# When the second gather, the first scatter and the embedding's product are written among the experts

## The chip, the cores and the metric

The kernel runs on one core of one Trainium2 chip. The metric is the device time of one execution, in microseconds (us), as the median of several runs. TensorE does the matrix products, VectorE (DVE), ScalarE (ACT) and GpSimd (POOL) the rest, and SyncE (SP) issues the transfers from the memory of the chip.

## The reference

Two layers of an encoder over 512 tokens of width 1024, in float32. Each layer has a token mixer, then a routed mixture of 16 experts, then a gated embedding. The change touches the last two:

```python
logits = jnp.einsum('bsd,de->bse', h, w_router)
aff = jax.nn.softmax(logits, axis=-1)
vals, idx = lax.top_k(aff.transpose(0, 2, 1), cap)      # cap = 64 tokens for each expert
xg = h[bidx, idx]
h1 = jnp.einsum('becd,edf->becf', xg, w1)               # w1, w3, w2: 1024 x 1024 for each expert
h3 = jnp.einsum('becd,edf->becf', xg, w3)
out = jnp.einsum('becf,efd->becd', jax.nn.silu(h1) * h3, w2) * vals[..., None]
x = x + jnp.zeros_like(h).at[bidx, idx].add(out)
...
ple_gate = jax.nn.sigmoid(rmsnorm(x, norm_ple[i]) @ ple_gate_w[i])
x = x + ple_gate * (p[i] @ ple_w[i])                    # p: 512 x 256, ple_w: 256 x 1024
```

Each expert has 12 MB of weights, and they are read once in each layer.

## The kernel before, in words

Tokens lie on the 128 partitions in four chunks, `x[:, c, :]`. The weights of an expert come as 1 MB tiles (`w_tile`, L565), four for each of `w1` and `w3`, into a ring of 15 slots (tag `s8`) that other tiles share. SP issues the loads in one queue, in order; a load waits until its slot is free.

The expert stage of a layer goes like this.

- Experts 0 to 3 (L806) each gather their own tokens (`gather_one`), do their products (`hidden`) and the product with `w2` (`down`), whose results stay in `obs`, one slot of the ring.
- `gather(ga, 4, 6)` (L820) gathers the tokens of experts 4 to 9 into `xgA`. It makes a mask `sel` from the positions (L710) and then, in eight steps, one for each 128 columns of `x`, splits a scaled `x` into a high and a low half (`xh` on ACT, `xl` on DVE, two buffers each), multiplies both with the mask on TensorE (eight matmuls, L720) and copies the result out of its bank.
- The loop over experts 4 to 15 (L835) calls `hidden` for each. Per expert: for `w1` and then `w3`, eight values of `k`, two halves (L738). The trace has two records for each of these 32 matmuls, 64 for an expert and 8 for a weight tile. After a quarter of an expert's products, `between` transposes the expert before it (L753) into the slot `kept`. Then tanh on ACT (L744) and two operations on DVE (L745, L746).
- Ahead of expert 7 (`GATHER_B`, L836) stands the gather of experts 10 to 15 into `xgB`. Behind expert 7 stand two calls of `scatter` (L846), which add the outputs in `obs` to `x`; each calls `where`, which makes a mask `sv` on DVE (L690), transposes it on TensorE (L693) into a bank of tag `T`, and multiplies it with the affinities (L698). `T` has two banks, and the transposes of `between` use it too.
- Behind expert 11 (`PLE_AT`, L847) stands the product of the embedding, `pw`: it loads `p` and two halves of `ple_w` through the same ring (L828), splits each into a high half (ACT, L95) and a low half (DVE, L831) and does eight groups of six matmuls (L150).
- After expert 15 come `where` for the last six pairs (L865) and the products with `w2` of experts 4 to 15 (L900) with their scatter.

The order of the instructions of each engine isn't that of the text. A planner goes through the whole program with a model of the chip's times; among the instructions whose inputs and slots are there it gives an engine the one that stands first in the program. The slots of one tag are handed out in the program's order. `issue_after` queues instructions behind a given one.

Of the kernel before, what the change touches and what calls it, by code (L numbers as in the profile page):

```python
# [10 lines left out]
F32 = mybir.dt.float32  # L11
# [8 lines left out]
P = 128  # L20
D = 1024
S = 512
NE = 16
CAP = 64
NEARLY = 6

ONE = 4
NA_ = 6
RING = 15
BLOCKED = 4  # L30
EARLY_END = ONE * 8 + BLOCKED * 4 - 4
GATHER_B = 7

PLE_AT = 11
SPL = 3
GTB = 1
S0B = 2
# [26 lines left out]
def trunk(ctx, tc, a, out, L=2, dbg=None):  # L64
# [15 lines left out]
    x = const.tile([P, 4, D], F32, name="x")  # L80
# [13 lines left out]
    def acopy(o, i, scale=1.0):  # L94
        sc.activation(o, i, AF.Copy, scale=scale)  # L95

    def bc(ap, n):
        return ap.unsqueeze(2).to_broadcast([P, ap.shape[1], n])
# [83 lines left out]
    for l in range(L):  # L182
# [263 lines left out]
        with tc.tile_pool(name=f"na{l}", bufs=2, side="right", reuse_waits="tile") as ap_:  # L446
# [3 lines left out]
            for pr in range(4):  # L450
                pts = []
                for hh_ in range(2):
# [4 lines left out]
                    for c in range(4):  # L457
# [16 lines left out]
                        n = NCH[c]  # L474
# [90 lines left out]
        def w_tile(src):  # L565
            i = nw[0]
            nw[0] += 1
            j = (i - START) % (RING + NEARLY)
            early = j < NEARLY and START <= i < EARLY_END
            if i in (0,) + GATED:  # L570
                nw[1] = gates[1 + (i >= GATED[0]) + (i >= GATED[1])]
            t = ((fw2 if j < EF else fw) if early else s8).tile([P, 2, D], F32, tag="w" if early else "s8", name="w")
            with tc.issue_after(nw[1].ins):
                d = dma(t, src.rearrange("p (k n) -> p k n", k=2))
                if START <= i < CHAIN:
                    nw[1] = d
            return t
# [71 lines left out]
        xg = gather_one(0)  # L649
# [52 lines left out]
                ve.tensor_scalar(val[r, :], ps[r, ee:ee + 1], 0.5, None, ALU.mult)  # L702
            return svT, val

        def gather(pool, e0, n):

            xg = pool.tile([P, 8, n * CAP], F32, tag="xg", bufs=1, name="xg")
            s = ga.tile([P, 4, n, CAP], F32R, tag="sel", bufs=1, name="sel")
            for c in range(4):
                ve.tensor_tensor(s[:, c], bc(pos[:, c, e0:e0 + n], CAP), iota.unsqueeze(1).to_broadcast([P, n, CAP]), ALU.is_equal)  # L710
            for k in range(8):
                xh = ga.tile([P, 4, P], F32R, tag="xh", name="xh")
                xl = ga.tile([P, 4, P], F32R, tag="xl", name="xl")
                for c in range(4):
                    xv = x[:, c, k * P:(k + 1) * P]
                    sc.activation(xh[:, c, :], xv, AF.Identity, scale=rx[:, c:c + 1])
                    ve.scalar_tensor_tensor(xl[:, c, :], xv, rx[:, c:c + 1], xh[:, c, :].bitcast(F32), ALU.mult, ALU.subtract)
                ps = psS.tile([P, n * CAP], F32, tag="S", name="gat")
                for i in range(8):
                    pe.matmul(ps, (xh if i % 2 == 0 else xl)[:, i // 2, :], s[:, i // 2].rearrange("p a b -> p (a b)"),  # L720
                              start=(i == 0), stop=(i == 7))
                if k % 2:
                    sc.activation(xg[:, k, :], ps, AF.Identity, scale=g_moe[:, k:k + 1])
                else:
                    ve.tensor_scalar(xg[:, k, :], ps, g_moe[:, k:k + 1], None, ALU.mult)
            return xg

        def hidden(e, xg, new=None, between=None):


            t13 = []
            for wsrc in (a["moe_w1"], a["moe_w3"]):
                ps = psA.tile([P, S], F32, tag="A", name="t13")
                for k in range(8):
                    if k % 2 == 0:
                        w = w_tile(wsrc[l, e, k // 2])
                    for hf in range(2):
                        products.append(pe.matmul(ps[hf * 64:(hf + 1) * 64, :], xg(k), w[:, k % 2, hf * S:(hf + 1) * S],  # L738
                                                  start=(k == 0), stop=(k == 7)))
                    if between and k == 3 and not t13:  # L740
                        between()
                t13.append(ps)
            u = ep.tile([P, S], F32, tag="u", bufs=1, name="u")
            sc.activation(u, t13[0], AF.Tanh, scale=0.5)  # L744
            ve.scalar_tensor_tensor(u, u, 1.0, t13[0], ALU.add, ALU.mult)  # L745
            ve.tensor_tensor(u, u, t13[1], ALU.mult)  # L746

            def turn():
                last = products[-1]
                tp = psT.tile([P, 4, 2, CAP], F32, tag="T", name="gT")  # L750
                with tc.issue_after(last.ins):
                    for q in range(4):
                        pe.transpose(tp[:, q].rearrange("p a b -> p (a b)"), u[:, q * P:(q + 1) * P], ident)  # L753
                gT = new() if new else ep.tile([P, 4, 2, CAP], F32, tag="gT", bufs=GTB, name="gT")
                acopy(gT, tp)
                return gT

            return turn

        def down(e, gT, ob):  # L760
            po = psA.tile([P, S], F32, tag="A", name="po")
            for k in range(8):
                if k % 2 == 0:
                    w = w_tile(a["moe_w2"][l, e, k // 2])
                for hf in range(2):
                    pe.matmul(po[hf * 64:(hf + 1) * 64, :], gT[:, k % 4, k // 4, :], w[:, k % 2, hf * S:(hf + 1) * S],  # L766
                              start=(k == 0), stop=(k == 7))
            r = slice(e % 2 * 64, e % 2 * 64 + 64)
            acopy(ob[r, 0:S], po[0:64, :])
            ve.tensor_copy(ob[r, S:D], po[64:128, :])  # L770

        def scatter(pr, ob):

            svT, val = where(pr)
            for hf in range(2):
                oh = qp.tile([P, S], F32R, tag="oh", bufs=OHB, name="oh")
                ol = qp.tile([P, S], F32R, tag="oh", bufs=OHB, name="ol")
                o = ob[:, hf * S:(hf + 1) * S]
                sc.activation(oh, o, AF.Identity, scale=val)
                ve.scalar_tensor_tensor(ol, o, val, oh.bitcast(F32), ALU.mult, ALU.subtract)  # L780
                for c in range(4):
                    ps = psS.tile([P, S], F32, tag="S", name="sca")
                    pe.matmul(ps, svT[:, c * P:(c + 1) * P], oh, start=True, stop=False)
                    pe.matmul(ps, svT[:, c * P:(c + 1) * P], ol, start=False, stop=True)
                    xv = x[:, c, hf * S:(hf + 1) * S]
                    ve.tensor_tensor(xv, ps, xv, ALU.add)

        obs, products = [], []
# [15 lines left out]
        gTs, pw = [], []  # L804

        for e in range(ONE):  # L806
# [3 lines left out]
            if e < ONE - 1:  # L810
                with tc.issue_after(products[-1].ins):
                    xg = gather_one(e + 1)
            else:
# [3 lines left out]
                gt = ExitStack()  # L817
                ga = gt.enter_context(tc.tile_pool(name=f"ga{l}", bufs=2, reuse_waits="tile"))
            down(e, gT, obs[e // 2])
        xgA = gather(ga, ONE, NA_)  # L820
        rt.close()
        st, xt_, pt_ = ExitStack(), ExitStack(), ExitStack()

# [9 lines left out]

        turn = None
        for e in range(ONE, NE):  # L835
            if e == GATHER_B:  # L836
                xgB = gather(xt_.enter_context(tc.tile_pool(name=f"x{l}", bufs=1, side="right", reuse_waits="tile")), ONE + NA_, NE - ONE - NA_)
            if e == ONE + NA_:
                gt.close()
                pp = pt_.enter_context(tc.tile_pool(name=f"ple{l}", bufs=2, reuse_waits="tile"))  # L840
            i = (e - ONE) % NA_
            xg = xgA if e < ONE + NA_ else xgB
            turn = hidden(e, lambda k: xg[:, k, i * CAP:(i + 1) * CAP], kept, turn and (lambda turn=turn: gTs.append(turn())))
            if e == GATHER_B:
                for pr in range(BLOCKED // 2):
                    scatter(pr, obs[pr])  # L846
            if e == PLE_AT:  # L847

                pT_ = load_s(a["p"][l], 2)
                for hf in range(2):  # L850
                    w = load_s(a["ple_w"][l, hf], 2)
                    pw.append(pp.tile([P, 4, S], F32, tag="pw", name="pw"))
                    for c in range(4):
                        ps = psO.tile([P, S], F32, tag="O", name="pw")
                        cs_ = slice(c * P, (c + 1) * P)
                        mm3(ps, [((pT_[0][:, k, cs_], pT_[1][:, k, cs_]), (w[0][:, k, :], w[1][:, k, :])) for k in range(2)])
                        acopy(pw[hf][:, c, :], ps, 0.5)
# [254 lines left out]
```

## Time and profile before

| | |
|---|---|
| median of three runs | 1950.42 us (1944.68 to 1953.8) |
| the profiled execution, its own time | 1943.66 us |
| its span, first to last instruction | 1941.9 us |
| busy: TensorE, DVE, ACT, POOL | 1876.7, 782.3, 593.0, 84.3 us |
| moved by DMA | 486.60 MB, 251 GB/s over the span |

The busy time of TensorE is 97% of the span. Matmuls are pipelined and their ends are modelled, so this says that it seldom stands quite still, not that it runs at its peak. The mean granted clock is 0.987 of full speed.

### The profile page before, as it was taken

Reading aid. Unit: us, or ns where it says so; the run is one execution under the profiler, and the core shown is the slowest. Engines: PE = TensorE matmul, PEld = TensorE weight load, DVE = VectorE, ACT = ScalarE, POOL = GpSimd, SP = SyncE. Lnnn points to the kernel's source line nnn. Section 1 sums busy time; section 2 is a strip of 40 time slices with the busy share of each in tenths; the row PEclk is TensorE's granted clock in tenths of the full one; section 3 lists DMA queues with packets and bytes.
Section 4 is the critical chain, followed back from the end, with each engine's and each line's share of the span. In section 5 each row is a group of like instructions: output and inputs, shape, how many; then the busy total and the mean of one; then the engine's idle time right before and its main releaser. Section 6 shows DMA issues by size and latency. Waiting matters only on the chain.

```text
span 1941.9 us, 25362 instructions
## 1 busy us (share of the span) xinstructions
PE 1876.7 (97%) x10028; PEld 1195.3 (62%) x10028; DVE 782.3 (40%) x1662; ACT 593.0 (31%) x1219; POOL 84.3 (4%) x156
## 2 busy tenths in 40 slices
PE   7999999999999999999899999999999999999995
PEld 7776777883354333666687677788734533336664
DVE  4656353444233310323756554444442422112346
ACT  4646443320132110221436454423101410212222
POOL 0022110000000000000000221100000000000000
PEclk9999999999999999999999999999999999999998
DMA  5220323488989999977412103236799899999781
GB/s 165 66 76 23 111 77 108 180 347 334 395 358 379 427 426 427 426 309 311 157 44 76 47 25 119 78 106 239 298 396 385 346 400 427 426 426 379 303 335 66
DMA packets 80997, 486.60 MB, mean 251 GB/s; under 512 B 9200, under 2 KB 11760, under 8 KB 30448
## 3 DMA queue, kind: packets, MB, share of 16 engines
q1 hardware_dynamic: 78000, 478.71, 62.3%
q10 hardware_dynamic: 2880, 6.29, 1.0%
q8 instruction: 79, 1.29, 0.3%
q14 instruction: 38, 0.31, 0.0%
HBM read 482.87 MB, written 2.10 MB: 250 GB/s over the span
## 4 chain that ended last, share of the span: by engine, by line
PE 88%; DVE 5%; DMA 4%; ACT 2%; issue 1%; SPq 0%; DVEq 0%; ACTq 0%
PE t L738 19%; PE po L900 9%; PE op L150 5%; PE xo L241 5%; PE pg L150 4%; DMA w<-in_moe_w_dram 3%; PE po L766 3%; PE sca L915 3%; PE gat L720 2%; PE vp L241 2%; PE o L430 2%; PE tokp L150 2%; PE gat L636 2%; PE pw L150 1%; PE s L410 1%; PE tp L423 1%
## 5 line engine op out<-in xcount | busy, mean ns | idle before, releaser
L738 PE MATMUL t<-w,xg 128*64 128x512 f32 x2048 | 459.2, 597 | 3.9 <-DMA w<-in_moe_w_dram 2.2
L738 PEld LDWEIGHTS t<-w,xg 128*64 128x64 f32 x2048 | 141.6, 137 | 279.9 <-issue 263.6
L192 DVE TENSOR_TENSOR wl<-raw,wh 128x1024 fp32r<-128x1024 f32 (+2 forms) x110 | 127.7, 1161 | 158.5 <-ACT wh L95 157.8
L900 PE MATMUL po<-s,s 128*64 128x256 f32 x1536 | 190.0, 385 | 0.0
L900 PEld LDWEIGHTS po<-s,s 128*64 128x64 f32 x1536 | 109.4, 138 | 60.5 <-issue 7.9
L95 ACT ACTIVATE wh<-raw 128x1024 fp32r<-128x1024 f32 (+2 forms) x110 | 110.8, 1007 | 116.9 <-PE xo L241 30.8
L150 PE MATMUL pg<-s,hp 128*128 128x512 f32 x384 | 101.3, 406 | 1.1 <-ACT hp L95 1.1
L745 DVE SCALAR_TENSOR_TENSOR u<-u,t 128x512 f32<-128x512 f32 x32 | 22.0, 687 | 189.6 <-ACT u L744 189.5
L746 DVE TENSOR_TENSOR u<-u,t 128x512 f32<-128x512 f32 x32 | 21.9, 685 | 161.6 <-PE t L738 161.6
L150 PEld LDWEIGHTS pg<-s,hp 128*128 128x128 f32 x384 | 68.5, 188 | 24.7 <-issue 7.7
L241 PE MATMUL xo<-wh,s 128*128 128x512 f32 x256 | 80.8, 392 | 0.0
L150 PE MATMUL op<-s,wh 128*128 128x512 f32 x256 | 80.1, 392 | 0.0
L906 ACT ACTIVATE oh<-po,val 128x256 fp32r<-128x256 f32 x48 | 22.8, 475 | 170.0 <-PE po L900 169.5
L907 DVE SCALAR_TENSOR_TENSOR oh<-po,val,oh 128x256 fp32r<-128x256 f32 x48 | 23.2, 484 | 118.6 <-ACT oh L906 118.5
L95 ACT ACTIVATE s<-gT 128x512 f32<-128x512 f32 x24 | 14.3, 596 | 182.7 <-PE gT L753 182.7
L915 PEld LDWEIGHTS sca<-oh,svT 128*128 128x128 f32 x384 | 51.0, 189 | 16.0 <-issue 9.6
L915 PE MATMUL sca<-oh,svT 128*128 128x256 f32 x384 | 59.5, 292 | 0.3 <-ACT oh L906 0.2
L766 PE MATMUL po<-w,gT 128*64 128x512 f32 x256 | 59.5, 602 | 0.0
L417 ACT ACTIVATE p<-s,nm 128x512 f32<-128x512 f32 x64 | 43.9, 686 | 50.1 <-DVE nm L414 47.7
L420 POOL TENSOR_SCALAR p<-p,rs 128x512 f32<-128x512 f32 x64 | 44.4, 696 | 338.4 <-DVE rs L419 310.1
L414 DVE TENSOR_REDUCE nm<-s 128x1 f32<-128x512 f32 x64 | 44.2, 690 | 33.4 <-PE s L410 23.7
L744 ACT ACTIVATE u<-t 128x512 f32<-128x512 f32 x32 | 19.1, 598 | 124.6 <-PE t L738 124.6
(478 smaller groups left out, 3217.2 us busy)
## 6 DMA issues: line engine op xcount, KB each, us to landing
w<-in_moe_w_dram SPq DMA_DIRECT2D x288, 1024.0 KB, 11.1
s<-in_moe_w_dram SPq DMA_DIRECT2D x96, 1024.0 KB, 10.9
raw<-in_w_in_dram SPq DMA_DIRECT2D x48, 512.0 KB, 3.5
raw<-in_w_out_dram SPq DMA_DIRECT2D x16, 512.0 KB, 3.5
s<-in_ple_gate_w_dram SPq DMA_DIRECT2D x8, 1024.0 KB, 10.2
bias<-in_bias_dram ACTq DMA_DIRECT2D x16, 320.0 KB, 2.9
raw<-in_w_v_dram SPq DMA_DIRECT2D x8, 512.0 KB, 3.5
raw<-in_w_mla_o_dram SPq DMA_DIRECT2D x8, 512.0 KB, 3.5
```

The costliest lines, as they stand in the source:

```text
L95: sc.activation(o, i, AF.Copy, scale=scale)
L150: pe.matmul(ps, s_, m_, start=(i == 0), stop=(i == n - 1))
L192: ve.tensor_sub(wl, raw, wh.bitcast(F32))
L241: pe.matmul(ps[c], s_[2 * i + k][:, cs_], m_[:, k, :], start=(i + k + j == 0), stop=(i == 3 and k == 1 and j == 2))
L414: ve.tensor_reduce(nm, s, AX.X, ALU.max, negate=True)
L417: sc.activation(pr_, s, AF.Exp, bias=nm, accum_out=sm)
L420: gp.tensor_scalar(pr_, pr_, rs, 1.0, ALU.mult, ALU.mult)
L430: pe.matmul(o[hh_ * 64:(hh_ + 1) * 64, :], vm[:, j, h * 64:(h + 1) * 64], pts[hh_][:, j, :], start=(j == 0), stop=(j == 3))
L738: products.append(pe.matmul(ps[hf * 64:(hf + 1) * 64, :], xg(k), w[:, k % 2, hf * S:(hf + 1) * S], start=(k == 0), stop=(k == 7)))
L766: pe.matmul(po[hf * 64:(hf + 1) * 64, :], gT[:, k % 4, k // 4, :], w[:, k % 2, hf * S:(hf + 1) * S], start=(k == 0), stop=(k == 7))
L900: pe.matmul(po[ee * CAP:(ee + 1) * CAP, :], gTs[2 * n + ee][:, k % 4, k // 4, :], ws[ee][:, k, :], start=(k == 0), stop=(k == 7))
L915: pe.matmul(ps[:, j, :], sT[:, (c + j) * P:(c + j + 1) * P], o, start=(i == 0), stop=(i == len(parts) - 1))
```

## The change

The second gather becomes a generator that is advanced by one step after each half of `w1` and of `w3` of experts 8 and 9, eight steps. The two scatters move from behind expert 7 to ahead of expert 12, and the embedding's product from behind expert 11 to behind expert 13. The first gather is used up at once, as before.

```diff
-GATHER_B = 7
-PLE_AT = 11
+GATHER_B = 8
+SCATTER = 12
+PLE_AT = 13
...
-        def gather(pool, e0, n):
-            xg = pool.tile([P, 8, n * CAP], F32, tag="xg", bufs=1, name="xg")
+        def gather(xg, e0, n):
             s = ga.tile([P, 4, n, CAP], F32R, tag="sel", bufs=1, name="sel")
...
-            return xg
+                yield
+
+        def gathered(pool, n):
+            return pool.tile([P, 8, n * CAP], F32, tag="xg", bufs=1, name="xg")
-        def hidden(e, xg, new=None, between=None):
+        def hidden(e, xg, new=None, between=None, steps=None):
...
                     if between and k == 3 and not t13:
                         between()
+                    if steps and k % 4 == 3:
+                        next(steps, None)
...
-        xgA = gather(ga, ONE, NA_)
+        xgA, steps = gathered(ga, NA_), None
+        for _ in gather(xgA, ONE, NA_):
+            pass
...
         for e in range(ONE, NE):
+            if e == SCATTER:
+                for pr in range(BLOCKED // 2):
+                    scatter(pr, obs[pr])
             if e == GATHER_B:
-                xgB = gather(xt_.enter_context(tc.tile_pool(name=f"x{l}", ...)), ONE + NA_, NE - ONE - NA_)
+                xgB = gathered(xt_.enter_context(tc.tile_pool(name=f"x{l}", ...)), NE - ONE - NA_)
+                steps = gather(xgB, ONE + NA_, NE - ONE - NA_)
...
-            turn = hidden(e, ..., turn and (lambda turn=turn: gTs.append(turn())))
-            if e == GATHER_B:
-                for pr in range(BLOCKED // 2):
-                    scatter(pr, obs[pr])
+            turn = hidden(e, ..., turn and (lambda turn=turn: gTs.append(turn())), steps)
```

## Rows read from the trace of the kernel before

**Rows 1.** Stretches of layer 0: us, busy by engine (PE first), clock, DMA share, GB/s.
```profile
520.00:573.00 53.00, 53.00 (x256) 24.63 (x254) 21.28 (x61) 17.08 (x49) 0.00 (x0) 1.00 0.85 335
573.00:602.00 29.00, 29.00 (x142) 16.31 (x140) 11.66 (x32) 10.52 (x30) 0.00 (x0) 1.00 0.93 357
602.00:615.00 13.00, 13.00 (x64) 4.42 (x62) 0.69 (x1) 1.20 (x2) 0.00 (x0) 1.00 0.97 408
...
700.00:708.00 8.00, 4.68 (x12) 2.78 (x12) 4.09 (x4) 0.79 (x2) 0.00 (x0) 0.76 1.01 425
708.00:739.00 31.00, 31.00 (x127) 12.64 (x128) 1.38 (x2) 5.65 (x10) 0.00 (x0) 0.95 1.01 426
...
774.00:781.00 7.00, 5.04 (x24) 1.28 (x21) 0.69 (x1) 0.00 (x0) 0.00 (x0) 1.00 1.01 428
781.00:823.00 42.00, 41.97 (x340) 29.64 (x340) 13.75 (x38) 10.70 (x23) 0.00 (x0) 1.00 1.01 426
```

**Rows 2.** Chain of waits, layer 0, 680 to 785: start, us, what.
```profile
700.64 2.37 DVE s L831 x2
...
711.48 1.58 PE pw L150 x6
...
738.10 0.59 PE gT L753 x4
738.69 13.88 PE t L738 x64
...
758.35 19.56 DMA w<-in_moe_w_dram
...
777.95 1.96 PE t L738 x8
```

**Rows 3.** Chain of waits, layer 1, 1630 to 1745.
```profile
1718.67 19.56 DMA w<-in_moe_w_dram
...
1738.27 1.96 PE t L738 x8
```

**Rows 4.** DMA issues of 540 to 800: count, KB each, us to landing.
```profile
w<-in_moe_w_dram SPq DMA_DIRECT2D x86, 1024.0 KB, 12.5
...
s<-in_ple_w_dram SPq DMA_DIRECT2D x2, 512.0 KB, 14.6
...
s<-in_p_dram SPq DMA_DIRECT2D x1, 512.0 KB, 17.9
```

**Rows 5.** TensorE in order of time, expert 7: start, us, line, operation.
```profile
618.46 0.66 PE L753 MATMUL gT<-ident,u 128*128 128x128 f32 x4
618.96 0.60 PE L693 MATMUL tp<-ident,sv 128*128 128x128 f32 x4
```

**Rows 6.** DVE in order of time, end of expert 11; idle before in brackets.
```profile
700.03 0.69 DVE L746 TENSOR_TENSOR u<-u,t 128x512 f32<-128x512 f32 x1 [5.55 <-PE t L738]
700.64 3.49 DVE L831 TENSOR_TENSOR s<-s,s 128x1024 fp32r<-128x1024 f32 x3
```

**Rows 7.** DVE in order of time, expert 4: the second mask.
```profile
564.29 1.96 DVE L710 TENSOR_TENSOR sel<-pos,iota 128x384 fp32r<-128x384 f32 x4
```

**Rows 8.** TensorE by line, 577 to 597 us: count, busy us, mean ns.
```profile
L720 PE MATMUL gat<-sel,xh 128*128 128x384 f32 x32 | 10.9, 346 | 0.0
L720 PE MATMUL gat<-sel,xl 128*128 128x384 f32 x32 | 10.9, 344 | 0.0
```

**Rows 9.** SP's issues in order of time, during the token mixer of layer 0.
```profile
302.88 0.37 SPq L954 DMA_DIRECT2D grow<-in_g_mix_dram  x1
```

**Rows 10.** DVE in order of time, expert 8: a mask.
```profile
642.91 0.89 DVE L690 TENSOR_TENSOR sv<-pos,iota 128x128 f32<-128x128 f32 x4
```

**Rows 11.** SP's issues in order of time around the embedding's loads.
```profile
678.69 0.33 SPq L828 DMA_DIRECT2D s<-in_p_dram  x1
682.12 3.76 SPq L828 DMA_DIRECT2D s<-in_ple_w_dram  x2
688.99 69.69 SPq L574 DMA_DIRECT2D w<-in_moe_w_dram  x32
```

More of the change, by code (lines that the diff above doesn't have):

```diff
@@ L835, in trunk @@
         for e in range(ONE, NE):
+            if e == SCATTER:
+                for pr in range(BLOCKED // 2):
+                    scatter(pr, obs[pr])
             if e == GATHER_B:
-                xgB = gather(xt_.enter_context(tc.tile_pool(name=f"x{l}", bufs=1, side="right", reuse_waits="tile")), ONE + NA_, NE - ONE - NA_)
+                xgB = gathered(xt_.enter_context(tc.tile_pool(name=f"x{l}", bufs=1, side="right", reuse_waits="tile")), NE - ONE - NA_)
+                steps = gather(xgB, ONE + NA_, NE - ONE - NA_)
             if e == ONE + NA_:
@@ L842, in trunk @@
             xg = xgA if e < ONE + NA_ else xgB
-            turn = hidden(e, lambda k: xg[:, k, i * CAP:(i + 1) * CAP], kept, turn and (lambda turn=turn: gTs.append(turn())))
-            if e == GATHER_B:
-                for pr in range(BLOCKED // 2):
-                    scatter(pr, obs[pr])
+            turn = hidden(e, lambda k: xg[:, k, i * CAP:(i + 1) * CAP], kept, turn and (lambda turn=turn: gTs.append(turn())), steps)
             if e == PLE_AT:
```

## The prediction

> **What bounds the kernel now.** I looked first for the one stretch of each layer that the change touches, the products of experts 4 to 15 with `w1` and `w3` (L738), with the busy time by stage [rows 1], then followed the chain of waits through it, in layer 0 and in layer 1 [rows 2, 3]. What the reader is to see in the stages: TensorE is shown as busy nearly throughout, and from 602 us on the transfers run at 408 to 428 GB/s with a DMA share of 0.97 to 1.01, to the end of the stage. So there are two resources that are both nearly full, and which one sets the end has to be worked out. A weight tile is 1 MB [rows 4], at 427 GB/s 2.46 us; an expert's eight tiles take 19.6 us to move. TensorE needs 13.88 us for an expert and 0.59 us for its transposes [rows 2], 14.47 us together. It can be slower than the transfers only because other work lies between the experts: the second gather, the first scatter, the embedding's product.
>
> Three numbers fix the end. Expert 7 starts 3.5 us (16 of 64 records) before the transposes at 618.46 [rows 5], at 615.0. DVE's last operation for expert 11 starts at 700.03, as soon as the expert's last product is there [rows 6]: 85.0 us for five experts (5 x 14.47 = 72.4) and the scatter, so the scatter costs TensorE 12.6. From 700.0 to the transposes at 738.10 lie expert 12, a quarter of expert 13 (17.3 us and 0.6) and the embedding's product, so the product costs 38.1 - 17.9 = 20.2 us. Of these 8 x 1.58 = 12.6 are its matmuls [rows 2]. The other 7.6 are a stall: the low halves of its operands stand on DVE behind expert 11's last operation, 2.37 us for the first two [rows 2, 6], and the granted clock is then 0.76 of full speed for 8 us and 0.95 for 31 us (a part of it at 1.2 instead of 2.4 GHz), 3.5 us of work lost [rows 1].
>
> TensorE alone would so end the stage at 700.0 + 20.2 + 4 x 14.47 = 778.1. The last tile lands at 758.35 + 19.56 = 777.91 and is used up at 779.91 [rows 2]. Before the change the transfers set the end, by some 2 us. Layer 1 repeats this: last tile at 1738.23, end at 1740.2 [rows 3].
>
> **The change, part by part.** No matmul, copy or transfer is added or taken away. Everything is in the order.
>
> *The gather in steps.* Where an instruction stands in the program isn't where it is issued: the planner issues what is ready when an engine is idle in its plan. Before, the gather stands ahead of expert 7, and its mask is made at 564.29, during expert 4 [rows 7]; its 64 matmuls run in 577 to 597, during expert 5 [rows 8]. How far can that go? A load that stands behind the whole expert stage (L954) is issued at 302.88, ahead of it [rows 9]; masks of the last pairs' `where`, which stands behind expert 15, are made at 642.91, during expert 8 [rows 10]. The gather's tiles (`sel`, `xh`, `xl`, and the `S` bank) have no other user between the first gather and expert 9. So I expect its steps to be taken just as early as before, in experts 5 and 6: cost and gain nothing. The other bound is that the steps stay where they are written; that is a rival below.
>
> *The scatter.* It can't run ahead in the same way. Its transposes take `T` banks, which are handed out in the order of the program behind expert 6's transposes, and indeed they start right after those, at 618.96 [rows 5]. Behind expert 11 it will start after expert 10's, in expert 11. So 12.6 us of TensorE's work moves from experts 7 and 8 to 11 and 12. The tile `obs` is kept four experts longer, one ring slot of 15; as TensorE will then be waiting for tiles, the ring is not what holds the transfers, and I cost this at nothing. If that cover is gone, one tile less ahead costs at most 2.46 us.
>
> *The embedding's product.* Its three half-MB loads [rows 4] come in SP's queue behind expert 11's tiles (678.69 and 682.12, the next weight at 688.99) [rows 11]; they pass sixteen weight tiles and go behind expert 13's. So experts 12 and 13 get their tiles 3.7 us earlier, experts 14 and 15 at the old times. The 20.2 us of TensorE's time move with it. Its stall stays, I think: the last DVE operation of expert 13 will stand ahead of the low halves as that of expert 11 did. Between a stall of 0 and one of 7.6 us I take 7.6, the value of this very row.
>
> **The sum.** The transfers already run at their full rate from 615 us, so no reordering of TensorE can make the last tile land before 777.9. Counting back, expert 13's last tile lands 16 tiles (39.3 us) and the three loads (3.7 us) earlier: 777.9 - 43.0 = 734.9. TensorE could be done with expert 13 at 615.0 + 7 x 14.47 + 12.6 = 728.9, so it waits, some 8 us in all, first in expert 10, where the scatter no longer gives the transfers time. Expert 13 ends at 734.9 + 2.0 = 736.9. Then come the product with its stall, 20.2, and two experts, 28.9: 786.0. Before it was 779.9, so 6.1 us more. In layer 1: 1738.2 - 43.0 + 2.0 + 49.1 = 1746.3 against 1740.2, 6.1 too. The point is that 49.1 us of TensorE's work are left behind expert 13, against 43.0 us of transfers. The stage that follows keeps TensorE busy without a gap and in 781 to 823 us has its weights in time, 41.97 of 42 us [rows 1], so nothing is given back there.
>
> Two layers: 12.2 us. The profiled execution took 1943.66 us (span 1941.9), so 1955.9. The three runs shown have a median of 1950.42, 6.8 above it; to the median I predict 1962.6.
>
> **Rivals.**
> *A: the gather stays where it is written* (experts 8 and 9). For it: that is what the diff says. Against it: [rows 7 to 10]. Then the transfers are not held up during experts 5 and 6. In 573 to 602 us they move 357 GB/s instead of 427 and in 602 to 615 us 408 [rows 1], 5.3 us lost, which would be won. Expert 13 then ends at 731.6 and the stage at 780.7, 0.8 us later than before; if some of what is lost in 520 to 573 us, at 335 GB/s, is won too, 8 us in all, TensorE itself sets the end, 778.1. Both layers: 1947 to 1952, no change.
> The Trainium skill, Trace Analysis, Identifying Performance Opportunities, says that a kernel with several regimes may improve if these are interleaved. By that rule the gather, spread over experts that wait for transfers, would bring 5.3 us a layer, 1940. The rows bear it out for the idle transfers, but not for where the gather would run.
>
> *B: the order is as I forecast, but the product doesn't stall,* because its loads have landed long before. The work behind expert 13 is 41.5 us, less than 43.0; the transfers set the end as before: 1950. From a stall of over 1.5 us on it is slower. Against it: the stall is in DVE's order, not in the landing [rows 6].
>
> *C, the other side: the gather runs late and the stall is gone.* TensorE alone ends the stage at 778.1 - 7.6 = 770.5; the last tile lands 5.3 to 8 us earlier, at 770 to 773, and is used up 2 us behind that: 5 to 8 us less a layer, 1934 to 1940. It needs both; it decides as soon as the stall is under 2 us with the gather in experts 8 and 9.
>
> *D: waiting cools the clock.* In expert 10 TensorE waits some 0.7 us for each tile. The nearest row is 774 to 781 us, 5.04 of 7 us busy at a granted clock of 1.00 [rows 1], and there it cost nothing. At half the clock eight records take some 3.7 us against 2.46 for a transfer; a drop that comes again behind expert 13, as long as the one of the stall, would cost 3.5 us more a layer: 1970.
> [...]
>
> **How the numbers follow.** The forecast has 0.52, A 0.14, B 0.14, C 0.10, D 0.10. Its own range is 1956 (no half clock: 2 x 3.5 less) to 1968 (in each layer one ring tile less ahead: 2 x 2.46 more). The range for 8 in 10 is 1944 to 1972: it takes in A, B and D and leaves out C. A measurement of this kernel can tell about 0.5% (9.8 us) from no change. Slower by more: D and most of the forecast, 0.55. Within: A, B, the low part of the forecast, 0.33. Faster: C and a little of A, 0.12.
>
> **What would show it.** Right: the gather's first matmul still near 577 us; the scatter's transposes in expert 11, near 680; waits for weight tiles in experts 10 and 13, some 8 us; the embedding's first product near 737 with a wait for DVE and a lower clock after it; the last expert some 8 us behind the landing of its last tile. Wrong: the gather's matmuls between tiles of experts 8 and 9 (A, C); no wait of the embedding's product for DVE (B, C); transfers that pause between 740 and 775 us, held up by the loads' slots (worse than I say).

## The result and the profile after

The changed kernel takes 1960.94 us (median of seven runs, 1957.5 to 1969.49), the kernel before in the same session 1945.11 (1938.13 to 1953.8): 1.008 times as long, with a 95% interval of 1.006 to 1.010. 15.8 us were lost.

The profiled execution of the changed kernel is the longest of its seven: 1969.49 us, span 1967.7, 25.8 us more than the span before. So I first set the starts of the same instructions of the two traces side by side, to see where the 25.8 arise. "The stretch" is from the first product of expert 7 to the last of expert 15.

| part of the span | layer 0 | layer 1 |
|---|---|---|
| up to expert 5 in layer 0; in layer 1 its router and first gathers | +4.2 | +4.6 |
| the stretch (before 164.37 and 164.09, after 169.88 and 170.08 us) | +5.5 | +6.0 |
| the products with `w2`, expert 15's last product to the last of them (`po`, their bank; 166.24 and 166.64; 170.02 and 170.01) | +3.8 | +3.4 |
| from there to the token mixer of layer 1 | -1.7 | |

The first line has nothing to do with the change, as the last section shows; without its 8.8 us there remain 17.0, near the 15.8 of the medians. The second line is what I had worked out as 6.1 a layer. The third I had put at nothing. The fourth is the granted clock: 0.83 in 1030 to 1040 us of the kernel before, 1.00 at the same place after (10 x 0.17 us).

The stages of layer 0 after the change (columns as in [rows 1]; all up to expert 7 stands 4.24 us later than before, and where a time is given "on the clock of before", these are taken off):

```profile
577.00:606.00 29.00, 29.00 (x144) 16.19 (x141) 11.90 (x32) 10.52 (x30) 0.00 (x0) 1.00 0.91 359
606.00:619.00 13.00, 13.00 (x64) 4.48 (x62) 0.69 (x1) 1.20 (x2) 0.00 (x0) 1.00 1.01 408
619.00:659.00 40.00, 40.00 (x190) 13.63 (x188) 4.12 (x6) 3.58 (x6) 0.00 (x0) 1.00 1.01 426
659.00:687.00 28.00, 24.01 (x107) 7.12 (x104) 2.06 (x3) 1.19 (x2) 0.00 (x0) 1.00 1.01 427
687.00:735.00 48.00, 48.00 (x225) 19.17 (x223) 20.20 (x45) 7.39 (x12) 0.00 (x0) 1.00 1.01 427
735.00:740.00 5.00, 3.95 (x20) 0.97 (x16) 0.00 (x0) 0.22 (x1) 0.00 (x0) 1.00 1.01 415
740.00:749.00 9.00, 5.75 (x16) 3.01 (x12) 4.09 (x4) 3.55 (x4) 0.00 (x0) 0.74 1.02 426
749.00:776.00 27.00, 27.00 (x111) 11.45 (x112) 1.38 (x2) 5.38 (x9) 0.00 (x0) 0.96 1.01 427
776.00:790.00 14.00, 13.63 (x66) 4.35 (x60) 1.01 (x2) 1.19 (x2) 0.00 (x0) 1.00 1.01 427
790.00:833.00 43.00, 41.77 (x314) 28.70 (x315) 12.83 (x37) 8.99 (x15) 0.00 (x0) 0.96 0.92 372
```

The reader is to see two things. From 619 us to the end of the stretch the transfers run at 426 or 427 GB/s (415 in 735 to 740), as before, so no time was won on them. And TensorE now stands still where it was full before: 4 of 28 us in 659 to 687 (experts 10 and 11), and again at 735 to 749, there with a clock of 0.74. The first two rows answer to the second and third of [rows 1]: the gather still holds the transfers at 359 GB/s. It hasn't moved: its first matmul runs at 581.25, 577.01 on the clock of before, and TensorE's groups by line in 577 to 606 are those of [rows 8]:

```profile
L721 PE MATMUL gat<-sel,xh 128*128 128x384 f32 x32 | 10.9, 346 | 0.0
L721 PE MATMUL gat<-sel,xl 128*128 128x384 f32 x32 | 10.9, 344 | 0.0
```

The chain of waits shows what TensorE waited for (columns as in [rows 2]; its lines are L743 for the products, L760 for the transposes of `between`, L695 for those of the scatter, L152 for `pw`, L840 for the low halves on DVE):

```profile
664.94 19.56 DMA w<-in_moe_w_dram
...
684.55 1.94 PE t L743 x8
686.48 0.59 PE gT L760 x4
687.07 0.44 PE tp L695 x4
...
718.94 19.56 DMA w<-in_moe_w_dram
738.50 0.04 issue
738.54 1.96 PE t L743 x8
...
742.27 1.23 DVE s L840
743.50 0.04 issue
743.54 1.93 PE pw L152 x5
...
779.18 10.47 PE t L743 x48
```

Before, such a row of a DMA ended the stretch [rows 2]. Now one ends expert 13: its last tile lands at 738.50, 734.3 on the clock of before, where I had written 734.9. Then come the stall, the product and two experts. The last 48 records run without a gap to 789.65, 785.4 on the clock of before; I had written 786.0.

Three more views of the stall, with what ended the idle time in brackets. TensorE in order of time:

```profile
736.11 1.94 PE L743 MATMUL t<-w,xg 128*64 128x512 f32 x8 [0.55 <-DMA w<-in_moe_w_dram]
738.54 1.94 PE L743 MATMUL t<-w,xg 128*64 128x512 f32 x8 [0.50 <-DMA w<-in_moe_w_dram]
742.14 0.50 PE L152 MATMUL pw<-s,s 128*128 128x512 f32 x1 [1.66 <-ACT s L97]
743.54 1.92 PE L152 MATMUL pw<-s,s 128*128 128x512 f32 x5 [0.90 <-DVE s L840]
746.14 2.93 PE L152 MATMUL pw<-s,s 128*128 128x512 f32 x6 [0.69 <-ACT pw L97]
```

and ACT, which makes the high halves:

```profile
739.78 1.06 ACT L97 ACTIVATE s<-s 128x1024 fp32r<-128x1024 f32 x1 [7.01 <-DMA s<-in_p_dram]
741.04 1.06 ACT L97 ACTIVATE s<-s 128x1024 fp32r<-128x1024 f32 x1 [0.20 <-DMA s<-in_ple_w_dram]
```

and DVE, which makes the low halves from them:

```profile
740.53 0.69 DVE L753 TENSOR_TENSOR u<-u,t 128x512 f32<-128x512 f32 x1 [7.04 <-PE t L743]
741.13 3.49 DVE L840 TENSOR_TENSOR s<-s,s 128x1024 fp32r<-128x1024 f32 x3
```

The waits are about as long as before, 3.25 us (1.66 + 0.90 + 0.69), and cost TensorE 3.4 us more by the clock (9 x 0.26 + 27 x 0.04 in the stages above). But the first two have another cause. Since TensorE now uses each tile as it lands, the embedding's loads, which stand behind expert 13's tiles in SP's queue, land just behind them: `p` at 739.8, the first half of `ple_w` at 741.0. Before, DVE's order was what held the product [rows 6]; now it is the landing and the splitting that follows it. The second low half, for which the product's second matmul waits, starts at 742.27 in the chain, and the high half that it is made from is ready only at 742.10 (741.04 + 1.06). DVE's operation of expert 13, which still stands ahead, costs under 0.2 us.

### The profile page after: what moved, and what is told of

It reads as the page before. It is cut to its first block, busy times and chain, and to the rows that moved or that the text cites. A ratio compares the mean times of both kernels' runs of the same rounds, so it can differ in the third digit from the quotient of the medians.

```text
span 1967.7 us, 25365 instructions
## 1 busy us (share of the span) xinstructions
PE 1892.3 (96%) x10028; PEld 1202.9 (61%) x10028; DVE 782.6 (40%) x1662; ACT 592.9 (30%) x1219; POOL 84.3 (4%) x156
## 4 chain that ended last, share of the span: by engine, by line
PE 85%; DMA 8%; DVE 5%; ACT 2%; issue 1%; SPq 0%; DVEq 0%; ACTq 0%
PE t L743 16%; PE po L910 9%; DMA w<-in_moe_w_dram 6%; PE op L152 4%; PE xo L243 4%; PE pg L152 4%; PE po L773 3%; PE sca L925 3%; PE gat L721 2%; PE vp L243 2%; PE o L432 2%; PE tokp L152 2%; PE pw L152 1%; PE s L412 1%; PE tp L425 1%; PE latp L152 1%
## 5 line engine op out<-in xcount | busy, mean ns | idle before, releaser
L743 PE MATMUL t<-w,xg 128*64 128x512 f32 x2048 | 463.0, 598 | 11.7 <-DMA w<-in_moe_w_dram 10.1
L743 PEld LDWEIGHTS t<-w,xg 128*64 128x64 f32 x2048 | 140.6, 137 | 292.8 <-issue 258.1
L152 PE MATMUL pg<-s,hp 128*128 128x512 f32 x384 | 100.9, 406 | 1.1 <-ACT hp L97 1.1
L152 PEld LDWEIGHTS pg<-s,hp 128*128 128x128 f32 x384 | 68.6, 188 | 24.1 <-issue 6.2
L152 PE MATMUL op<-s,wh 128*128 128x512 f32 x256 | 80.1, 392 | 0.0
## 6 DMA issues: line engine op xcount, KB each, us to landing
w<-in_moe_w_dram SPq DMA_DIRECT2D x288, 1024.0 KB, 12.6
```

What stands on the lines that cost most here:

```text
L152: pe.matmul(ps, s_, m_, start=(i == 0), stop=(i == n - 1))
```

## The experiments

Ratios are against the kernel before, run on the same chip, with a 95% interval. Where the gather is pinned, that is queued behind products of experts 8 and 9, it lies in the stretch; there the comparison goes from expert 5's first product to expert 15's last ("the long stretch", 206.25 and 205.97 us before, 211.76 and 211.95 after).

**The parts of the change: e1, e2, e3, e8**

*e1_gather_whole*: the change, but the gather in one piece ahead of expert 7 again.

```
-GATHER_B = 8
+GATHER_B = 7
-                steps = gather(xgB, ONE + NA_, NE - ONE - NA_)
+                for _ in gather(xgB, ONE + NA_, NE - ONE - NA_):
+                    pass
```

> The changed kernel with its gather as before, in one piece ahead of expert 7; scatter ahead of expert 12 and product behind expert 13 stay. My theory: the place in the text doesn't move the gather, since it is taken as soon as its tiles are free; so the gather's matmuls run in the same places of TensorE's order, and from expert 7's first product to expert 15's last it takes 169.9 us in layer 0, as in the changed kernel (169.88), a ratio to the kernel before of 1.008. Rival: the eight steps cost something of their own (waits on the halves, a later copy-out); then this run is nearer to the 164.4 us and the ratio 1.00 of the kernel before.

Measured: 1958.4 us, 1.0062 [1.0043, 1.0081]. The order of TensorE's instructions is that of the changed kernel, and the stretch takes 170.08 in layer 1. In layer 0 it takes 166.51, as there the clock doesn't fall behind the stall, though its three waits are the same 1.7, 0.9 and 0.7 us (the stall lies in 735 to 740 here, and the row behind it is at 1.00 where the changed kernel has 0.74):

```profile
735.00:740.00 5.00, 2.13 (x7) 1.26 (x8) 3.77 (x4) 2.71 (x4) 0.00 (x0) 1.00 1.02 426
740.00:749.00 9.00, 9.00 (x40) 3.75 (x39) 0.00 (x0) 1.79 (x3) 0.00 (x0) 1.00 1.01 427
781.00:824.00 43.00, 41.44 (x326) 29.06 (x328) 14.41 (x39) 9.52 (x18) 0.00 (x0) 1.00 1.00 418
```

So cutting up the gather is worth nothing, and the clock's 3.4 us come in some executions and not in others. The third row is the start of the products with `w2`, at 1.00 too; they take 168.30 and 168.33 here, against 170.02 and 170.01 with the row of 0.96.

*e2_product_alone*: the kernel before with the product's new place alone.

```
-PLE_AT = 11
+PLE_AT = 13
```

> The kernel before with the embedding's product behind expert 13 and nothing else changed. My theory: what counts is the work of TensorE that is left behind the point to which the transfers have held it. With the scatter still early TensorE reaches expert 13's end at 728.9 us on the clock of the kernel before, waits for the tile of 734.9, and ends the stage at 786: 6 us a layer slower, as with the whole change; stretch of experts 7 to 15 170 us, ratio 1.005 to 1.009. Rival: the loss is shared by the scatter, which also moved; then some 167 us and a ratio near 1.003.

Measured: 1963.02 us, 1.0102 [1.0073, 1.0131]; the stretch 170.71 and, with no fall of the clock, 166.63. The product's place alone brings the whole loss, with the scatter still in experts 7 and 8. TensorE waits for tiles about as long as in the changed kernel (there 5.0 us in ten waits), here in experts 12 and 13 alone. By releaser, in 655 to 790 us (us in all, times, longest):

```profile
PE t L738 <- DMA w<-in_moe_w_dram: 5.6, 11, 0.6
```

*e3_product_back*: the change with the product behind expert 11.

```
-PLE_AT = 13
+PLE_AT = 11
```

> The changed kernel with the product back behind expert 11; only the scatter has moved (ahead of expert 12). My theory: TensorE is held by the transfers until the scatter begins, 16 records into expert 11; the tile there is at hand at 680.8 us and used up at 682.7. Behind it lie 10.8 us of expert 11, 12.6 of scatter, 20.2 of product with its stall and 57.9 of four experts, 101.5 us, to 784.2: 4.3 us a layer slower than before (779.9), stretch 168.7 us, ratio 1.004 to 1.006. Rival: the scatter's move is free, as the transfers leave it room, and only the product's place costs: 164.4 us and a ratio of 1.000.

Measured: 1951.56 us, 1.0028 [1.001, 1.0045]; the stretch 163.40 and 164.35. My number for the stretch, 168.7, was wrong. I had added the scatter's 12.6 us and the product's 20.2 in front of the last experts; but the scatter of expert 12 and the product run into one another. DVE in order of time, at the place where [rows 6] shows three low halves in a row:

```profile
699.31 1.23 DVE L840 TENSOR_TENSOR s<-s,s 128x1024 fp32r<-128x1024 f32 x1 [0.28 <-ACT s L97]
700.45 0.68 DVE L753 TENSOR_TENSOR u<-u,t 128x512 f32<-128x512 f32 x1
701.04 1.28 DVE L793 TENSOR_TENSOR x<-sca,x 128x512 f32<-128x512 f32 x2
702.24 1.22 DVE L840 TENSOR_TENSOR s<-s,s 128x1024 fp32r<-128x1024 f32 x1
```

While DVE does these, TensorE has the scatter's matmuls (it waits 1.0 us for L793 and 0.4 for L840), and the clock stays at 1.00. But for these waits the stall is gone, and the product takes 30.5 us from first to last matmul, 35.9 before. Without the 7.6 us of the stall my 784.2 becomes 776.6, less than the 779.9 that the transfers had set; and TensorE does wait for the last two tiles again, 0.34 and 0.55 us. The loss of 0.28% is all in the products with `w2`, 170.1 in both layers.

*e8_product_14*: the change with the product behind expert 14, one execution.

```
-PLE_AT = 13
+PLE_AT = 14
```

> The changed kernel with the product behind expert 14 instead of 13. My theory: expert 14's last tile is at hand at 777.9 - 19.7 - 3.7 = 754.5 us and used up at 756.5; behind it lie 20.2 us of product and 14.5 of expert 15, to 791: 11 to 12 us a layer more than before, stretch of experts 7 to 15 175 to 176 us (164.4 before, 169.9 in the changed kernel); 3.5 less where the clock doesn't fall. Rival: the loss in the changed kernel is the scatter's or the shorter ring's, and doesn't grow with the product's place: 170 us.

Measured: 1967.8 us; the stretch 173.85 and 172.07, with 8.8 us of waits for tiles in 655 to 800 us where the changed kernel has 5.0. So the loss grows with the place of the product: behind expert 11 none, behind 13 5.5 to 6.0, behind 14 8.0 to 9.5. My sum gave 11 to 12 there, with one expert less (14.47 us) against eight tiles less (19.6): the way was right, the size missed. Part of the step from 11 to 13 is the stall, which e3 doesn't have.

**The gather where it is written: e4, e5**

*e4_pinned*: the steps are queued behind the products that they follow in the text.

```
                     if steps and k % 4 == 3:
-                        next(steps, None)
+                        with tc.issue_after(products[-1].ins):
+                            next(steps, None)
```

> The changed kernel with each step of the gather queued on TensorE behind the product it is written behind, so that it does run in experts 8 and 9. My theory: the transfers are then not held up during experts 5 and 6 (5.3 to 8 us won) and TensorE doesn't run dry in expert 10. The product's stall stays. From expert 5's first product to expert 15's last, 206.3 us before and 211.8 in the changed kernel, it takes 203.5 to 207; ratio to the kernel before 0.997 to 1.000. Rival: the loss comes from the late scatter and product alone, whatever the gather does: 211.8 us and 1.008.

Measured: 1943.94 us, 0.999 [0.997, 1.001]; the long stretch 205.40 and 206.44. The first matmul of the gather runs at 624.84, the steps lie between the experts' products. This is rival A, made on purpose: no change. The transfers get what the gather held up, and the late product takes it away again.

*e5_pinned_early*: besides, the scatter and the product earlier.

```
-SCATTER = 12
+SCATTER = 10
-PLE_AT = 13
+PLE_AT = 11
```

> The gather queued in experts 8 and 9 as in the run before, the scatter ahead of expert 10 and the product behind expert 11, two experts earlier than in the changed kernel. My theory: less work is left behind the points to which the transfers hold TensorE, so TensorE itself sets the end, at about its own sum with the stall partly covered: 774 to 778 us on the clock of the kernel before, 2 to 6 us a layer faster than it; from expert 5's first product to expert 15's last 201 to 205 us (206.3 before), ratio 0.994 to 0.998. Rival: with the gather pinned the place of scatter and product no longer matters; then it is as the run with the gather pinned alone, 205 to 206 us and 0.999.

Measured: 1939.25 us, 0.9968 [0.995, 0.9986]; the long stretch 204.51 and 204.93. It beats both kernels. In 573 to 602 us the transfers now run at their full rate, where [rows 1] has 357 GB/s:

```profile
573.00:602.00 29.00, 29.00 (x138) 9.84 (x134) 2.79 (x5) 2.39 (x4) 0.00 (x0) 1.00 1.01 426
602.00:615.00 13.00, 13.00 (x64) 4.37 (x62) 0.95 (x2) 1.19 (x2) 0.00 (x0) 1.00 1.01 428
```

The Trainium skill, Perfetto Trace Analysis, Identifying Performance Opportunities, says that stages with different limits may gain by being interleaved. These rows agree for the transfers. But of the 5.3 us a layer that rival A names as lost there, only 1.0 to 1.7 came out at the end, because behind it TensorE is the one that is full: it waits for no tile in 655 to 790 us, and the stall (2.63 us for DVE) is there again.

**The stall by itself: e6, e7, e9, e10, e11**

Here the embedding's loads and their splits are written an expert earlier (e6, e7), and besides the product's matmuls are queued behind the last product written before them (e9 to e11).

```
             xg = xgA if e < ONE + NA_ else xgB
+            if e == PLE_AT:
+                pT_ = load_s(a["p"][l], 2)
+                pws = [load_s(a["ple_w"][l, hf], 2) for hf in range(2)]
             turn = hidden(e, ...)
...
-                    w = load_s(a["ple_w"][l, hf], 2)
+                    w = pws[hf]
...
-                        mm3(ps, ...)
+                        with tc.issue_after(products[-1].ins):
+                            mm3(ps, ...)
```

*e6_pinned_loads*: e5 with the early loads.

> As the run with scatter ahead of 10 and product behind 11, and the three loads of the product with their splits written ahead of expert 11's products, so that DVE makes the low halves before expert 11's last operation. My theory: no stall and no lower clock behind it; TensorE's own sum is then 770.5 us on the clock of the kernel before, and the last tile, 5 to 8 us earlier than before, is used up at 772 to 775: 5 to 8 us a layer faster, stretch from expert 5 to expert 15 198 to 202 us, ratio 0.991 to 0.995. Rival: the stall is not on the path that sets the end once the transfers do; then no better than the run without this step.

Measured: 1947.94 us, 1.0009 [0.9995, 1.0023]; the long stretch 209.34 and 208.45, where I had written 198 to 202. The planner took not only the loads but the whole product an expert earlier, and the stall with it: TensorE waits 4.5 us for L841, the low halves. And the transfers fall back in 690 to 730 us, so that tiles are waited for later:

```profile
690.00:730.00 40.00, 35.48 (x141) 15.52 (x141) 7.84 (x16) 6.34 (x11) 0.00 (x0) 0.91 0.95 376
760.00:790.00 30.00, 26.19 (x120) 8.27 (x116) 2.75 (x4) 2.54 (x5) 0.00 (x0) 1.00 1.01 427
```

That slots of the ring, held by the early loads, are what kept the transfers back is argued, not tried.

*e7_before_loads*: the kernel before with the early loads.

> The kernel before with only that step: the product's three loads and splits written ahead of expert 11's products. My theory: before the change the transfers set the end of the stage (last tile 777.9 us), so taking the stall away from TensorE brings nothing here: stretch of experts 7 to 15 163.5 to 165 us (164.4 before), ratio 0.998 to 1.001. Rival: TensorE set the end, and 7.6 us of stall a layer come off: 157 us and 0.992.

Measured: 1952.31 us, 1.0027 [1.0009, 1.0044]; the stretch 164.57 and 164.72. It doesn't tell what it was made for: here too the product moved along with its loads, and the stall is as it was (2.6 us for DVE, the product 35.9 us). The next three keep the product in its place.

*e9_before_nostall*: e7 with the matmuls queued.

> The kernel before with the product's loads and splits ahead of expert 11's products, and now the product's matmuls queued behind expert 11's last one, since without that the planner moved the whole product up by an expert, stall and all. My theory: the stall is gone (the product with the experts between takes some 30 us from its first to its last matmul, 35.9 before), and the stage ends when it did, since the transfers set the end: stretch of experts 7 to 15 163.5 to 165 us, ratio 0.998 to 1.003. Rival: TensorE set the end: 157 us.

Measured: 1953.06 us, 1.0031 [1.0015, 1.0046]; the product takes 27.57 us, the stall is gone, and the stretch is 164.12 and 164.19, as before. TensorE's waits by releaser and the stage, in 740 to 785 and 740 to 780 us:

```profile
PE t L738 <- DMA w<-in_moe_w_dram: 4.8, 10, 0.7
...
740.00:780.00 40.00, 35.98 (x162) 10.86 (x158) 3.44 (x5) 2.99 (x5) 0.00 (x0) 1.00 1.01 427
```

What the stall gave back is spent on waiting for tiles. So before the change the transfers set the end of the stretch, as I had worked out from a difference of 2 us. The whole is slower all the same: in this profile the products with `w2` take 169.85 and 171.53 us, against 166.24 and 166.64 before; the last part of the account comes back to this.

*e10_after_nostall*: the change, without the stall in the same way.

> The changed kernel with the same step at expert 13: loads and splits ahead of its products, matmuls queued behind its last one. My theory: expert 13's last tile is then behind the three loads, at hand at 777.9 - 39.3 = 738.6 us and used up at 740.6; behind it lie 12.6 us of product without a stall and 28.9 of two experts, to 782.1: 2.2 us a layer slower than before where the changed kernel is 6 slower; stretch of experts 7 to 15 166 to 167 us, ratio 1.002 to 1.005. Rival: the loss comes from the work itself behind expert 13, not from the stall: 170 us as in the changed kernel.

Measured: 1952.73 us, 1.0032 [1.0019, 1.0045]; the stretch 168.18 and 167.39, the product 27.57 us. Of the 5.5 and 6.0 us that the change costs in the stretch, 1.7 and 2.7 go with the stall, 3.8 and 3.3 stay. They are in waits for tiles, 8.5 us in seventeen waits, all of them ahead of the product (which starts at 739.6). Behind it TensorE is full to the end of the stretch, 42.6 us, where I had 41.5; this and the rest of the 1.1 to 1.6 us above the 2.2 that I expected stay open:

```profile
718.00:740.00 22.00, 18.33 (x80) 5.23 (x77) 5.03 (x6) 2.25 (x3) 0.00 (x0) 1.00 1.01 427
740.00:788.00 48.00, 47.19 (x222) 21.21 (x222) 5.13 (x16) 8.86 (x15) 0.00 (x0) 1.00 1.01 427
```

*e11_pinned_nostall*: e5 without the stall, the same edit on e6.

> The fastest run so far (gather queued in experts 8 and 9, scatter ahead of 10, product behind 11) with the same step at expert 11. My theory: with the transfers no longer held up in experts 5 and 6 and no stall, the last tile is used up at 772 to 775 us on the clock of the kernel before: from expert 5's first product to expert 15's last 199 to 202 us (206.3 before, 204.5 in the run without this step), ratio 0.991 to 0.995. Rival: the loads' six slots of the ring hold the transfers up as in the run with the loads early and nothing queued; then 204 us or more.

Measured: 1941.84 us, 0.9977 [0.9962, 0.9992]; the long stretch 203.97 and 202.73, 0.5 and 2.2 better than e5, with intervals of the whole that overlap, and short of the 199 to 202 that I expected. TensorE waits for tiles at the end again:

```profile
750.00:780.00 30.00, 25.24 (x116) 8.04 (x112) 2.75 (x4) 2.88 (x5) 0.00 (x0) 1.00 1.01 427
```

## Why the prediction held, point by point

**The gather in steps: right.** It stays in experts 5 and 6, and e1 shows that its new form is worth nothing. e4 shows that where it runs and not where it is written is what counts: the same text, pinned, takes 0.999 of the time before.

**The scatter: right in its place**, and its cover held: its transposes run at 687.07 us, in expert 11, the transfers stay at 427 GB/s with `obs` kept longer, and e2, which leaves it where it was, loses as much as the whole change.

**The product: right, and the cause of the loss.** Behind expert 13 TensorE had more work left than the transfers, and e8, e2 and e3 follow that with the place. The pair without a stall on either side is e3 and e10 (whose loads are early): the stretch is 4.8 and 3.0 us longer with the product behind 13. The waits for tiles in front of it are 5.0 us in ten waits in the view by releaser, where I had some 8. Eight records that stand alone also take 1.94 us where in a run they take 1.74 (13.88 / 8), by my estimate some 2 us more over the ten. The end of expert 13 came when foreseen all the same, since the landing of its last tile sets it.

**The stall: right in size, wrong in cause.** I took 7.6 us, on the ground that "the stall is in DVE's order, not in the landing [rows 6]". After the change it is the landing: DVE's order costs under 0.2 us of it in the rows above. That its waits are as long as before, 3.25 us against 3.32, is luck. And it is no fixed term: its half, the clock, is missing in one layer of e1 and of e2 (3.6 and 4.1 us less), and nearly the whole goes where other matmuls fall into it (e3).

**The end of the transfers: right** for before (e9). Rival B, no stall and so no loss, is not what e10 shows: 3.3 to 3.8 us a layer are left. But to take the stall away e10 also takes the three loads out of the transfers behind expert 13, 39.3 us instead of 43.0, and TensorE's 41.5 are then the longer part by 2.2. B as I had it, with the loads behind expert 13's tiles and landed in time, wasn't tried; the rows of ACT above say that they can't land in time there.

**Rival D: wrong.** In 659 to 687 us eight of the nine groups of eight records wait 0.4 to 0.6 us for their tile, and the clock stays at 1.00:

```profile
679.67 1.94 PE L743 MATMUL t<-w,xg 128*64 128x512 f32 x8 [0.50 <-DMA w<-in_moe_w_dram]
682.19 1.94 PE L743 MATMUL t<-w,xg 128*64 128x512 f32 x8 [0.59 <-DMA w<-in_moe_w_dram]
```

The Trainium skill, TensorE: Matmul & The Clock Gate, Loop structure matters more than you think, has TensorE go cold where a long DMA wait stands between every two matmuls. The waits here are short, with eight records between them, and this trace doesn't show it for them.

**What follows the stretch: the term that failed.** I wrote "nothing is given back there" of a stage with TensorE full and its weights in time, and meant that it would take as long as before. It takes 3.8 and 3.4 us longer a layer. The runs have it in several orders of TensorE's instructions, and some with a fall of the clock shortly behind its start, which adds 1.6 to 1.7 us to each order (us):

| the order is that of | without the fall | with it |
|---|---|---|
| the kernel before, layer 1 | 164.93 (e6, layer 0) | 166.64 (before, layer 1), 166.56 (e4, layer 0) |
| the kernel before, layer 0 | 166.24 (before, layer 0), 166.19 (e10, layer 0) | 167.88 (e4, layer 1) |
| the changed kernel | 168.30 and 168.33 (e1) | 170.02 and 170.01 (the changed kernel) |

In layer 0, where the kernel before has no such fall, 1.7 us are the clock and 2.1 the order. In layer 1 the kernel before has the fall too, and the 3.4 us are the order:

```profile
1741.00:1783.00 42.00, 41.82 (x320) 29.32 (x322) 13.13 (x38) 9.08 (x15) 0.00 (x0) 0.96 1.01 426
```

The products with `w2`, the masks' transposes and the scatter stand otherwise in it; part of the loss is seen in the waits for ACT's `oh`, the high half of what the scatter adds. Here the changed kernel from expert 15 to the last `po` of layer 0:

```profile
PE sca L925 <- ACT oh L916: 1.3, 3, 0.6
```

and e10 in the same part, which takes 166.19 us there:

```profile
PE sca L928 <- ACT oh L919: 0.2, 1, 0.2
```

It isn't tied to one part of the change: e2, e3 and e7, which moves only three loads, have the changed kernel's order as well (168.4 in e7), and e4 and layer 0 of e10 have those of before. e9, which is the kernel before with its loads early and its product queued, is slower still (169.85, and 171.53 with the fall of the clock), with five such waits of 2.0 us in all. What tips the planner from one to the other stays open.

That the predicted total came within 1.7 us is partly luck. These 7.2 us in two layers were partly met by the 1.7 ahead of layer 1's mixer, and by a median of before that was 5.3 us lower than the one I started from: the loss in the medians is 15.8, I had 12.2.

## What to carry to other kernels

Where two resources are both nearly full, draw a line at each point of the schedule and compare what is left of each behind it; a piece of work that only one of them does belongs ahead of the point at which the other has less left, and moving it later costs the difference. Under a planner that takes whatever is ready, an edit of the text is a change only if the inputs or slots of the moved work come later: look in the trace at where such work is taken now, and pin it if it has to run later. And a stage that the edit doesn't touch may be planned anew all the same, here at 2 to 3 us of 166, so a change of a few tenths of a per cent has to be looked for stage by stage.

## What the runs showed of the chip that was not expected

The granted clock differs between executions of one order of instructions. From the router to expert 0's products the changed kernel has a row that e5, with the same work there, doesn't have. The changed kernel:

```profile
388.00:430.00 42.00, 41.49 (x225) 35.93 (x223) 15.45 (x29) 8.86 (x19) 0.00 (x0) 0.96 0.85 336
430.00:448.00 18.00, 17.31 (x117) 14.74 (x118) 7.20 (x24) 4.14 (x11) 0.00 (x0) 0.80 0.54 227
```

and e5:

```profile
430.00:448.00 18.00, 17.25 (x130) 11.86 (x131) 10.90 (x31) 4.13 (x11) 0.00 (x0) 1.00 0.65 261
```

The order of the instructions on TensorE, DVE and ACT is the same in both up to there. TensorE is as busy in both, 17.3 of 18 us, but at 0.80 and at 1.00; the part at 1.2 GHz makes 5.3 us of lost work (42 x 0.04 + 18 x 0.20), and expert 0 starts 4.6 us later (73.56 against 68.96 us from the first matmul into `xo`, ahead of the router). It is seen in both layers of the changed kernel's, of e6's and of e7's profile, in one layer of e4, e9 and e11, and in none of the others, so it follows neither the change nor the layer. The seven executions of the changed kernel have mean clocks from 0.982 (the profiled one, the slowest) to 0.989. One profiled execution may so stand 9 us off another by this alone; it is the first line of the table above.
